# Seven block products instead of eight for half the inner dimension of each MLP's first matrix, in a two-layer decoder trunk

## The chip, the cores and the metric

The kernel runs on one core of a Trainium2 chip. The metric is the device time of one execution in microseconds (us). The engines are TensorE (PE: matmuls; its weight loads are shown apart as PEld), VectorE (DVE), ScalarE (ACT), GpSimd (POOL) and SyncE (SP), whose queue issues most DMAs.

## The reference

Two groups of requests, a prompt of 1024 tokens and 8 x 8 sample tokens, go through two layers with shared weights, in fp32. Layer 0 mixes with gated linear attention (GLA), layer 1 with sliding-window attention; after each mixer comes the MLP that the change touches, then a gated per-layer input embedding (PLE). D_MODEL is 1024, D_FF 4096.

```python
def sq_relu_mlp(hn, w_up, w_down):
    return jnp.square(jax.nn.relu(hn @ w_up)) @ w_down

for i in range(DEPTH):                      # DEPTH = 2
    ...                                     # h = h + mixer(rmsnorm(h, norm_mix[i]))
    h = h + sq_relu_mlp(rmsnorm(h, w['norm_mlp'][i]), w['w_up'][i], w['w_down'][i])
    gate = jax.nn.sigmoid(rmsnorm(h, w['norm_ple'][i]) @ w['w_ple_gate'][i])
    h = h + gate * (p[i] @ w['w_ple'][i])
```

## The kernel before

Both groups are handled together: activations lie transposed, features on the 128 partitions and all T = 1088 tokens along the row. `h` is a list of KT = 8 such tiles, one per 128 features. A row of tokens is cut into the three chunks `CH` of 364, 362 and 362, each of which fits one PSUM buffer. PSUM has three buffers under the tag `mm`, three under `gx` and two under `gs`.

**Precision by three passes.** Every large matmul uses fp32r operands that are split in a high part (a cast on ACT) and a low part (the difference, on DVE). `mm3` (L160 to L165) issues three matmuls, high x high, high x low and low x high. So one 128 x 128 weight block against one chunk is three matmuls, each with its own weight load.

**Weights.** `plan` (L1084) lists all weight tiles in the order of use, each 128 x 512, four 128 x 128 blocks. `wfill` (L115) loads a tile into one of two `raw` buffers, casts it to one of five `hi` buffers (L139) and takes the difference into one of five `lo` buffers (L140). `wnext` (L143) keeps three tiles ahead of the one in use.

**out_proj** (L655) ends the mixer: for each `j` it multiplies, adds the residual to get `h[j]` (L652), adds its square to the norm's sum `acc` (L225, L226), and splits `h[j]` times the gain into a double tile in `hg` (L195 on ACT, L196 on DVE). `norm_end` makes `rb`, the reciprocal norm of each token, through a matmul with ones (L231) and a chain on DVE and ACT (L205 to L210). `rb` is applied after the matmul, so PE can begin the MLP before it is there.

**mlp** (L684) goes over FB = 8 blocks `fb` of the 4096 inner features, FT = 4 tiles of 128 in each. In the up part each `f` is 8 weight blocks x 3 chunks x 3 passes = 72 matmuls; the first `f` of all runs with the weight blocks outermost, so that it asks for the last `hg` late. Each chunk is then evacuated: DVE takes relu times `rb` out of PSUM (L703), ACT squares (L704) and casts (L705), and DVE takes the low part (L706); the result is `u`. In the down part each of eight `j` is 4 blocks x 3 chunks x 3 passes = 36 matmuls, and DVE adds the chunk to `h[j]` (L715). In the last `fb` each `h[j]` is squared, summed and split for the PLE.

**PLE.** A memory pool for its inputs stays open for the whole MLP. At `fb` 2 and 4 `ple_input` (L731) loads one 128 x 1088 tile of `p` each and splits it (L192 on ACT, L193 on DVE). The gate's evacuation (L755) is the first reader of the next `rb`.

**Order.** The program is written as straight code without explicit waits. When it is built, the instructions of each engine are put into one fixed order, by their dependences and by their order in the code, and the waits are added. On the chip each engine then works through its list in that order.

Of the kernel before, what the change touches and what calls it, by code (L numbers as in the profile page):

```python
# [11 lines left out]
F32 = mybir.dt.float32  # L12
F32R = mybir.dt.float32r
U8 = mybir.dt.uint8
AF = mybir.ActivationFunctionType
# [4 lines left out]
P = 128  # L20
# [15 lines left out]
NEG = -1e30  # L36
G_MIX0, G_MLP0, G_PLE0, G_KV, G_MIX1, G_MLP1, G_PLE1, G_FIN = range(8)
WMAX = 544
R = (slice(0, 64), slice(64, 128))


# [5 lines left out]
class Trunk:  # L47
# [67 lines left out]
    def wfill(self, n):  # L115

        while len(self.wtiles) < min(n, len(self.wplan)):
            k, src, width, gains = self.wplan[len(self.wtiles)]
            nc = self.nc
            if src is None:  # L120
                raw = self.rawpair[:, 1, :]
            elif len(src.shape) == 3:
                self.rawpair = self.double("G2", F32)
                self.load(self.rawpair[:, :, :width], src.rearrange("s p w -> p s w"))
                raw = self.rawpair[:, 0, :]
            else:
                raw = self.wp.tile([P, WMAX], F32, tag="raw", name=self.uid("raw"), bufs=2)
                self.load(raw[:, :width], src)
            hi = self.wp.tile([P, WMAX], F32R, tag="hi", name=self.uid("whi"), bufs=5)
            lo = self.wp.tile([P, WMAX], F32R, tag="lo", name=self.uid("wlo"), bufs=5)  # L130
            step = width // len(gains) if gains else width
            for i in range(width // step):
                s = slice(i * step, (i + 1) * step)
                if gains:
                    nc.scalar.activation(hi[:, s], raw[:, s], AF.Copy, scale=gains[i])
                    nc.vector.scalar_tensor_tensor(lo[:, s], raw[:, s], gains[i], hi[:, s].bitcast(F32),
                                                   op0=ALU.mult, op1=ALU.subtract)
                else:
                    nc.scalar.copy(hi[:, s], raw[:, s])  # L139
                    nc.vector.tensor_tensor(lo[:, s], raw[:, s], hi[:, s].bitcast(F32), op=ALU.subtract)  # L140
# [513 lines left out]

    def out_proj(self, key, xs, resid, gain, tags, after=None, begun=0):  # L655
        nc = self.nc
        self.norm_begin()
        self.hg = []
        for j in range(KT):
# [21 lines left out]
        self.norm_end()  # L681


    def mlp(self, layer, gain, utag, tags):  # L684
        nc = self.nc
        xs, rb = self.hg, self.rb
        self.norm_begin()
        self.hg = []
        pt = ("mm", "gx")
        for fb in range(FB):  # L690
            us = []
            if layer == 0:
                self.bias_copies(fb)
            if fb in (2, 4):
                self.ple_input(layer, fb // 2 - 1)
            for f in range(FT):
                ws = self.wtile([("up", layer, fb * FT + f, 0), ("up", layer, fb * FT + f, 1)])
                u = self.double(utag)

                def evac(c0, cn, ps):  # L700
                    s = slice(c0, c0 + cn)
                    t = self.t364()
                    nc.vector.scalar_tensor_tensor(t[:, :cn], ps, 0.0, rb[:, s], op0=ALU.max, op1=ALU.mult)  # L703
                    nc.scalar.activation(t[:, :cn], t[:, :cn], AF.Square)  # L704
                    nc.scalar.copy(u[:, 0, s], t[:, :cn])  # L705
                    nc.vector.tensor_tensor(u[:, 1, s], t[:, :cn], u[:, 0, s].bitcast(F32), op=ALU.subtract)  # L706
                self.gemm(ws, xs, evac, kouter=(fb == 0 and f == 0), tags=pt)
                us.append(u)
# [13 lines left out]
        self.norm_end()  # L722


    def ple_pool(self, layer):
        ctx = ExitStack()
        self.pl = ctx.enter_context(self.tc.tile_pool(name=f"pl{layer}", bufs=1))
        self.p = []
        return ctx
# [354 lines left out]
    def plan(self):  # L1084
# [16 lines left out]
        def rest(layer):  # L1101
# [3 lines left out]
            for j in range(begun, KT):  # L1105
                w.extend(two((f"wo{layer}", j), I[f"w_o{layer}"], j))
            for fb in range(FB):
                for f in range(FT):
                    w.extend(two(("up", layer, fb * FT + f), I["w_up"][layer], fb * FT + f))
# [25 lines left out]
    def run(self):  # L1135
# [7 lines left out]
        def keep(j, h, chunks):  # L1143
# [5 lines left out]
        with self.ple_pool(0):  # L1149
            self.mlp(0, G_PLE0, "G1", ("G2", "G3"))  # L1150
            self.sample_bias()
            self.ple(0, keep)
# [7 lines left out]
        with self.ple_pool(1):  # L1160
            self.mlp(1, G_PLE1, "G2", ("G3", "G1"))
            self.ple(1, scale)


@with_exitstack
# [96 lines left out]
```

## Time and profile before

| | us |
|---|---|
| median of 3 runs | 2738.29 (2736.81 to 2740.18) |
| the profiled execution | 2741.02 |
| its span, first to last instruction | 2738.9 |
| PE busy | 2706.5, 17217 matmuls |
| DVE busy | 1448.5 |
| ACT busy | 1065.8 |
| POOL busy | 128.0 |

The granted TensorE clock is 0.996 of full speed on average. Durations of single instructions can overlap with those of the next on the same engine: the mean durations of a group times its count are then more than its busy time, which counts each moment once. A line of a timeline reads: start, duration, engine, source line, operation, result and operands by name, shape, count, and in brackets the idle time before it and what ended it. A line of a window reads: the stretch, its length, and for each engine its busy time and number of instructions, then the granted clock, the DMA engines' share and GB/s.

### The profile page before, as it was taken

To read this page: it belongs to the slowest core of one execution; us is meant where nothing else is said; L and a number is where in the kernel's file an instruction comes from. 1 tells how busy PE (TensorE), PEld (TensorE's weight loads), DVE (VectorE), ACT (ScalarE), POOL (GpSimd) and SP (SyncE) were. 2 spreads that over 40 slices of the span, in tenths; PEclk is the share of its full clock that TensorE was granted. 3 is DMA by queue.
4 is the path that set the end of the run, shared out by engine and by line. 5 is a ranking of instruction groups with operands and counts; after the bars stand their busy time and mean duration, and the time that the engine had idled before them with its cause. 6 is when DMAs were issued, how large, how long until landed. Compare 5 with 4: busy or idle time off the path is not lost.

```text
span 2738.9 us, 43239 instructions
## 1 busy us (share of the span) xinstructions
PE 2706.5 (99%) x17217; PEld 2639.3 (96%) x17217; DVE 1448.5 (53%) x3481; ACT 1065.8 (39%) x2326; POOL 128.0 (5%) x154
## 2 busy tenths in 40 slices
PE   9999999999999999999999999999999999999997
PEld 8999999999999999999999887899999999999997
DVE  5788786453343343334654677653333333333687
ACT  5565575241122122114434666532221221222465
POOL 0000000001001000010000433200000000000000
PEclk9999999999999999999999999999999999999999
DMA  3121112211111121121122111221111111111152
GB/s 125 40 65 41 57 58 71 90 52 53 53 51 50 45 64 48 49 75 51 56 84 71 41 43 36 70 70 43 47 51 44 46 51 47 43 47 43 36 184 96
DMA packets 92783, 163.34 MB, mean 60 GB/s; under 512 B 11558, under 2 KB 30650, under 8 KB 92549
## 3 DMA queue, kind: packets, MB, share of 16 engines
q1 hardware_dynamic: 89637, 155.20, 18.6%
q10 hardware_dynamic: 1152, 4.46, 0.5%
q8 instruction: 135, 2.21, 0.3%
q0 software_dynamic: 1792, 0.92, 0.2%
q14 instruction: 67, 0.55, 0.1%
HBM read 145.95 MB, written 19.98 MB: 61 GB/s over the span
## 4 chain that ended last, share of the span: by engine, by line
PE 96%; DVE 2%; ACT 1%; issue 0%; DMA 0%; POOL 0%; DVEq 0%; SPq 0%; ACTq 0%; POOLq 0%
PE mm L163 22%; PE mm L164 22%; PE mm L165 22%; PE gx L165 7%; PE gx L164 7%; PE gx L163 7%; PE gx L523 2%; PE gx L1035 1%; PE gx L1021 1%; PE gx L552 1%; PE gx L547 1%; PE gs L1004 1%; PE gs L231 0%; PE gx L554 0%; PE gs L1005 0%
## 5 line engine op out<-in xcount | busy, mean ns | idle before, releaser
L163 PE MATMUL mm<-G,whi 128*128 128x362 f32 (+1 forms) x3416 | 1129.3, 331 | 6.2 <-ACT G L195 6.2
L165 PE MATMUL mm<-G,wlo 128*128 128x362 f32 (+1 forms) x3416 | 1127.7, 330 | 0.1
L164 PE MATMUL mm<-G,whi 128*128 128x362 f32 (+1 forms) x3416 | 1126.3, 330 | 0.0
L163 PEld LDWEIGHTS mm<-G,whi 128*128 128x128 f32 x3416 | 642.9, 188 | 12.7 <-ACT G L195 6.6
L164 PEld LDWEIGHTS mm<-G,whi 128*128 128x128 f32 x3416 | 643.2, 188 | 3.5 <-issue 1.7
L165 PEld LDWEIGHTS mm<-G,wlo 128*128 128x128 f32 x3416 | 642.6, 188 | 3.2 <-issue 1.6
L139 ACT CAST whi<-raw 128x512 fp32r<-128x512 f32 (+1 forms) x368 | 226.4, 619 | 659.1 <-PE mm L164 625.8
L165 PE MATMUL gx<-G,wlo 128*128 128x362 f32 (+1 forms) x1048 | 344.3, 329 | 0.0
L164 PE MATMUL gx<-G,whi 128*128 128x362 f32 (+1 forms) x1048 | 343.8, 328 | 0.0
L163 PE MATMUL gx<-G,whi 128*128 128x362 f32 (+1 forms) x1048 | 343.1, 328 | 0.0
L140 DVE TENSOR_TENSOR wlo<-raw,whi 128x512 fp32r<-128x512 f32 (+1 forms) x368 | 252.0, 690 | 66.1 <-ACT whi L139 65.5
L715 DVE TENSOR_TENSOR H<-H,mm 128x364 f32<-128x364 f32 (+1 forms) x256 | 136.2, 532 | 277.3 <-PE mm L165 276.0
L704 ACT ACTIVATE tmp<-tmp 128x362 f32<-128x362 f32 (+1 forms) x192 | 97.2, 507 | 461.5 <-DVE tmp L703 456.1
L165 PEld LDWEIGHTS gx<-G,wlo 128*128 128x128 f32 x1048 | 198.0, 189 | 0.0
L163 PEld LDWEIGHTS gx<-G,whi 128*128 128x128 f32 x1048 | 197.8, 189 | 0.0
L164 PEld LDWEIGHTS gx<-G,whi 128*128 128x128 f32 x1048 | 197.6, 189 | 0.0
L706 DVE TENSOR_TENSOR G<-tmp,G 128x362 fp32r<-128x362 f32 (+1 forms) x192 | 102.8, 536 | 157.4 <-ACT G L705 157.3
L703 DVE SCALAR_TENSOR_TENSOR tmp<-mm,rb 128x364 f32<-128x364 f32 (+1 forms) x128 | 68.6, 536 | 196.8 <-PE mm L165 196.8
L715 DVE TENSOR_TENSOR H<-H,gx 128x362 f32<-128x362 f32 x128 | 68.0, 531 | 140.9 <-PE gx L165 140.9
L225 ACT ACTIVATE tmp<-H 128x362 f32<-128x362 f32 (+1 forms) x126 | 63.6, 506 | 133.0 <-DVE H L652 74.6
L705 ACT CAST G<-tmp 128x362 fp32r<-128x362 f32 (+1 forms) x192 | 95.0, 496 | 5.8
L226 DVE TENSOR_TENSOR acc<-acc,tmp 128x362 f32<-128x362 f32 (+1 forms) x126 | 67.2, 535 | 36.2 <-ACT tmp L225 35.3
(254 smaller groups left out, 3002.0 us busy)
## 6 DMA issues: line engine op xcount, KB each, us to landing
raw<-in_w_up SPq DMA_DIRECT2D x128, 256.0 KB
raw<-in_w_down SPq DMA_DIRECT2D x128, 256.0 KB
G<-in_w_gate SPq DMA_DIRECT2D x24, 512.0 KB
raw<-in_w_o SPq DMA_DIRECT2D x32, 256.0 KB
raw<-in_w_q SPq DMA_DIRECT2D x24, 256.0 KB
x<-in_xT ACTq DMA_DIRECT2D x8, 544.0 KB
hd<-H SPq DMA_DIRECT2D x8, 544.0 KB
x<-hd SPq DMA_DIRECT2D x8, 544.0 KB
```

The lines of the kernel that those rows point to most:

```text
L139: nc.scalar.copy(hi[:, s], raw[:, s])
L140: nc.vector.tensor_tensor(lo[:, s], raw[:, s], hi[:, s].bitcast(F32), op=ALU.subtract)
L163: mm(out, lhsT=w[0], rhs=x[0], start=first, stop=False)
L164: mm(out, lhsT=w[0], rhs=x[1], start=False, stop=False)
L165: mm(out, lhsT=w[1], rhs=x[0], start=False, stop=last)
L225: nc.scalar.activation(sq[:, :cn], h[:, s], AF.Square)
L226: nc.vector.tensor_tensor(self.acc[:, s], self.acc[:, s], sq[:, :cn], op=ALU.add)
L703: nc.vector.scalar_tensor_tensor(t[:, :cn], ps, 0.0, rb[:, s], op0=ALU.max, op1=ALU.mult)
L704: nc.scalar.activation(t[:, :cn], t[:, :cn], AF.Square)
L705: nc.scalar.copy(u[:, 0, s], t[:, :cn])
L706: nc.vector.tensor_tensor(u[:, 1, s], t[:, :cn], u[:, 0, s].bitcast(F32), op=ALU.subtract)
L715: nc.vector.tensor_tensor(h[:, s], h[:, s], ps, op=ALU.add)
```

## The change

The up matrix of each MLP is no longer done one `f` at a time but in pairs of `f` (`up_pair`). Of the 8 inner blocks `k`, blocks 4 to 7 are multiplied as before. Blocks 0 to 3 go through Strassen's scheme in Winograd's form: the 2 output tiles, the 2 halves of the inner blocks (0, 1 and 2, 3) and the 2 halves of the tokens (HT = 544) form a 2 x 2 x 2 block product of seven products instead of eight. Each half of the tokens is taken in two chunks of CT = 272, one in an `mm` and one in a `gx` buffer.

- **Sums of activations.** `half_sums(i)` forms, for i = 0 and 1, the four sums of the token halves of `h[i]` and `h[i+2]`, split in high and low part, once per layer during out_proj (after `j` = 4 and 6). Three of the four lie in new memory (`st`), one in the second half of `hg[i]`, which therefore is split only for its first half.
- **Sums of weights.** `up_weights` forms the sums of weight blocks from tiles `a1` and `a2` on DVE, two instructions of 256 columns for each of the two sum tiles. The plan has per pair four loaded tiles as before and six split tiles, one of them half as wide: A1, S2S1, C1, S4S3, A22, C2.
- **Sums of products.** The groups of matmuls of a pair are, in order: A1 (12 matmuls), S2S1 (12), A1 and C1 (36), S2S1 (12), S4S3 (12), S4S3 and C1 (36), A22 and C2 (36), C2 (24). Two products are copied to memory on ACT (`p1`, `p5`), three sums are kept in `x`, `u3` and `p5` by DVE, and each `out` adds one of them to its group before relu.
- **Memory.** The sums of products use the buffer `wide` and that of `acc`, so `norm_begin` moves to the last `fb`. The pool for PLE inputs opens only there, in place of `st`, and both `ple_input` follow one another after the last up pair.

The first `f` no longer has a k-outer order. The diff, cut to its core:

```diff
+HT, CT = T // 2, T // 4
@@ wfill
-            if src is None:
+            if isinstance(gains, str):
+                raw, gains = self.up_weights(gains, src), None
+            elif src is None:
@@
+    def up_weights(self, which, src):
+        nc, st = self.nc, self.st
+        q = 2 * P
+        if which == "A1":
+            raw = self.a1 = st.tile([P, 512], F32, tag="a1", name=self.uid("a1"), bufs=1)
+            self.load(raw, src)
+            return raw
+        if which == "A22":
+            return self.a2[:, q:]
+        a1 = self.a1
+        s = st.tile([P, 512], F32, tag="sum", name=self.uid("sum"), bufs=2)
+        if which == "S2S1":
+            a2 = self.a2 = st.tile([P, 512], F32, tag="a2", name=self.uid("a2"), bufs=1)
+            self.load(a2, src)
+            nc.vector.tensor_tensor(s[:, q:], a2[:, :q], a2[:, q:], op=ALU.add)
+            nc.vector.tensor_tensor(s[:, :q], s[:, q:], a1[:, :q], op=ALU.subtract)
+            self.s2 = s
+        else:
+            nc.vector.tensor_tensor(s[:, q:], a1[:, :q], self.a2[:, :q], op=ALU.subtract)
+            nc.vector.tensor_tensor(s[:, :q], a1[:, q:], self.s2[:, :q], op=ALU.subtract)
+        return s
@@ out_proj
-            self.split(d, h, self.gain(gain, j), CH if j >= 6 else ((0, T),))
+            self.split(d, h, self.gain(gain, j), CH if j >= 6 else ((0, HT if j < 2 else T),))
             self.hg.append(d)
+            if j in (4, 6):
+                self.half_sums(j // 2 - 2, gain)
@@
+    def half_sums(self, i, gain):
+        nc = self.nc
+        h1, h2, g1, g2 = self.h[i], self.h[i + 2], self.gain(gain, i), self.gain(gain, i + 2)
+        tiles = [self.hg[i][:, :, HT:]] + [self.st.tile([P, 2, HT], F32R, name=self.uid("tx")) for _ in range(3)]
+        self.tx.append(tiles)
+        for c in (0, CT):
+            n1, n2 = slice(c, c + CT), slice(HT + c, HT + c + CT)
+
+            def part(which, t):
+                d = tiles[which]
+                nc.scalar.copy(d[:, 0, n1], t)
+                nc.vector.tensor_tensor(d[:, 1, n1], t, d[:, 0, n1].bitcast(F32), op=ALU.subtract)
+            t1, t2, b = (self.t364()[:, :CT] for _ in range(3))
+            nc.scalar.activation(b, h1[:, n1], AF.Copy, scale=g1)
+            nc.vector.scalar_tensor_tensor(t1, h1[:, n2], g1, b, op0=ALU.mult, op1=ALU.subtract)
+            part(0, t1)
...
+    def up_pair(self, layer, f, xs, us):
...
+        def out(i, half, x, pss):
+            u = us[i]
+            for c in range(2):
+                s = slice(half * HT + c * CT, half * HT + (c + 1) * CT)
+                t = self.t364()[:, :CT]
+                nc.vector.tensor_tensor(t, x[c], pss[c], op=ALU.add)
+                nc.vector.scalar_tensor_tensor(t, t, 0.0, rb[:, s], op0=ALU.max, op1=ALU.mult)
+                nc.scalar.activation(t, t, AF.Square)
+                nc.scalar.copy(u[:, 0, s], t)
+                nc.vector.tensor_tensor(u[:, 1, s], t, u[:, 0, s].bitcast(F32), op=ALU.subtract)
...
+        a1, s21 = nxt("A1"), nxt("S2S1")
+        ps = bank()
+        add(ps, take(a1, 0), lambda k: (xs[k], 0), True)
+        copies(p1, ps)
+        ps = bank()
+        add(ps, take(s21, 0), lambda k: (tx[k][1], 0), True)
+        sums(x, p1, ps)
+        ps = bank()
+        add(ps, take(a1, 2), lambda k: (xs[k + 2], 0), True, False)
+        c1 = nxt("C1")
+        add(ps, take(c1, 0, 4), lambda k: (xs[k + 4], 0))
+        out(0, 0, p1, ps)
+        ps = bank()
+        add(ps, take(s21, 2), lambda k: (tx[k][0], 0), True)
+        copies(p5, ps)
+        s43 = nxt("S4S3")
+        ps = bank()
+        add(ps, take(s43, 2), lambda k: (tx[k][2], 0), True)
+        sums(u3, x, ps)
+        sums(x, x, p5)
+        sums(p5, p5, u3)
+        ps = bank()
+        add(ps, take(s43, 0), lambda k: (xs[k + 2], HT), True, False)
+        add(ps, take(c1, 0, 4), lambda k: (xs[k + 4], HT))
+        out(0, 1, x, ps)
+        ps = bank()
+        add(ps, take(nxt("A22"), 0), lambda k: (tx[k][3], 0), True, False)
+        c2 = nxt("C2")
+        add(ps, take(c2, 0, 4), lambda k: (xs[k + 4], 0))
+        out(1, 0, u3, ps)
+        ps = bank()
+        add(ps, take(c2, 0, 4), lambda k: (xs[k + 4], HT), True)
+        out(1, 1, p5, ps)
@@ mlp
-        self.norm_begin()
         self.hg = []
+        self.pq = self.wide("pq")
+        self.xz = self.rs.tile([P, TP], F32, tag="acc", name=self.uid("xz"), bufs=1)
...
-            if fb in (2, 4):
-                self.ple_input(layer, fb // 2 - 1)
-            for f in range(FT):
...
+            for f in range(0, FT, 2):
+                us += [self.double(utag) for _ in range(2)]
+                self.up_pair(layer, fb * FT + f, xs, us[f:])
+            if fb == FB - 1:
+                self.norm_begin()
+                self.stx.close()
+                self.ple_open(layer)
```

Left out of the diff are the rest of `half_sums` (three more sums of the same kind), helpers inside `up_pair`, the new lines of `plan`, and `ple_open`, which opens the pool and calls `ple_input` twice.

More of the change, by code (lines that the diff above doesn't have):

```diff
@@ new lines, in up_pair, with bank, take, add @@
+    def up_pair(self, layer, f, xs, us):
+        nc, rb = self.nc, self.rb
+        tx = self.tx
+        def bank():
+            return [self.ps(tag)[:, :CT] for tag in ("mm", "gx")]
+        def take(key, i, count=2):
+            hi, lo = key
+            return [(hi[:, k * P:(k + 1) * P], lo[:, k * P:(k + 1) * P]) for k in range(i, i + count)]
+        def add(pss, ws, x, first=False, stop=True):
+            for c, ps in enumerate(pss):
+                for k, w in enumerate(ws):
+                    d, off = x(k)
+                    off += c * CT
+                    self.mm3(ps, w, (d[:, 0, off:off + CT], d[:, 1, off:off + CT]), first and k == 0,
+                             stop and k == len(ws) - 1)
+        nxt = lambda which: self.wnext(("up", layer, f, which))
+        two = lambda t, i: [t[:, (2 * i + c) * CT:(2 * i + c + 1) * CT] for c in range(2)]
+        p1, p5, x, u3 = two(self.pq, 0), two(self.pq, 1), two(self.xz, 0), two(self.xz, 1)
+        def out(i, half, x, pss):
[8 more added lines that the diff above has]
+                nc.vector.tensor_tensor(u[:, 1, s], t, u[:, 0, s].bitcast(F32), op=ALU.subtract)
+        def copies(t, pss):
+            for c in range(2):
+                nc.scalar.copy(t[c], pss[c])
+        def sums(t, x, pss):
+            for c in range(2):
+                nc.vector.tensor_tensor(t[c], x[c], pss[c], op=ALU.add)
+        a1, s21 = nxt("A1"), nxt("S2S1")
[31 more added lines that the diff above has]
+        out(1, 1, p5, ps)
```

54 lines of the change are left out of this document (30 added, 24 removed).

## The prediction

> **What bounds the kernel now.** I read the page first: its busy times, and its chain of work that ended last.
>
> ```profile
> span 2738.9 us, 43239 instructions
> ...
> PE 2706.5 (99%) x17217; PEld 2639.3 (96%) x17217; DVE 1448.5 (53%) x3481; ACT 1065.8 (39%) x2326; POOL 128.0 (5%) x154
> ...
> PE 96%; DVE 2%; ACT 1%; issue 0%; DMA 0%; POOL 0%; DVEq 0%; SPq 0%; ACTq 0%; POOLq 0%
> ...
> L163 PE MATMUL mm<-G,whi 128*128 128x362 f32 (+1 forms) x3416 | 1129.3, 331 | 6.2 <-ACT G L195 6.2
> ```
>
> 96% of the chain is TensorE (PE), and most of that is the three matmul lines of `mm3`. The MLP is where the change lies, so next come windows over it and over stages that resemble what it will become.
>
> ```profile
> core 0: us, PE busy (x) PEld busy (x) DVE busy (x) ACT busy (x) POOL busy (x), PEclk, DMA share, GB/s
> 942.56:990.40 47.84, 47.84 (x291) 47.84 (x290) 19.18 (x33) 16.86 (x32) 0.00 (x0) 1.00 0.15 45
> 990.40:1038.20 47.80, 47.80 (x289) 47.80 (x289) 17.78 (x32) 5.35 (x9) 6.84 (x12) 1.00 0.21 55
> 65.00:440.00 375.00, 372.53 (x2739) 350.61 (x2738) 301.02 (x1099) 232.68 (x602) 2.84 (x5) 1.00 0.17 54
> 514.00:554.00 40.00, 40.00 (x242) 40.00 (x242) 14.70 (x26) 8.80 (x16) 0.00 (x0) 1.00 0.31 99
> 1278.00:1326.00 48.00, 48.00 (x289) 47.77 (x288) 37.80 (x65) 26.42 (x45) 0.00 (x0) 1.00 0.19 50
> 1719.35:1722.77 3.42, 3.42 (x24) 2.21 (x23) 1.58 (x7) 1.65 (x5) 0.98 (x1) 0.50 0.00 0
> ```
>
> The rows are: an up stage (four `f` of one `fb`), a down stage, the GLA layer, out_proj before the MLP, the last down stage, and a moment of attention. In the MLP PE never pauses, and VectorE (DVE) is busy 19.18 of 47.84 us, 40%. So time falls only if PE does less, and only until DVE or ScalarE (ACT) sets the pace instead.
>
> **The matmuls.** Per pair of `f` the old code issues 2x8x3x3 = 144 matmuls of 362.67 columns on average, 52,224 columns. The new one issues, for its eight groups, 12, 12, 36, 12, 12, 36, 36 and 24 matmuls of 272 columns: 180 matmuls, 48,960 columns, one sixteenth fewer. Whether a matmul is paid by its columns or by the piece decides the gain. 272-column matmuls of the same type stand in the trace: the V projection of head 0 (L389). For the old width I take the evacuations of the first `f` of `fb` 1 and 7.
>
> ```profile
> 37.18 0.29 PE L163 MATMUL mm<-whi,G 128*128 128x272 f32 x1
> ...
> 61.13 0.29 PE L163 MATMUL mm<-whi,G 128*64 128x272 f32 x1
> ```
>
> ```profile
> 659.73 0.54 DVE L703 SCALAR_TENSOR_TENSOR tmp<-mm,rb 128x364 f32<-128x364 f32 x1 [3.44 <-PE mm L165]
> ...
> 1233.77 0.54 DVE L703 SCALAR_TENSOR_TENSOR tmp<-mm,rb 128x364 f32<-128x364 f32 x1 [3.47 <-PE mm L165]
> ```
>
> Between the first two rows lie 8 blocks of 8x3 matmuls: 23.95 us / 192 = 124.7 ns each. Between the second two lie six `fb` of 576 matmuls: 574.04 / 3456 = 166.1 ns. Per column that is 0.4586 and 0.4580 ns: no price per piece is seen. Over two layers of 16 pairs, 4608 x 166.1 = 765.4 us becomes 5760 x 124.7 = 718.5 us: **46.9 us less**. Two neighbouring matmuls of the old width can stand up to 166.7 ns apart, which would make it 50; that is the bound below.
>
> The Trainium skill (TensorE: Matmul & The Clock Gate, "Wait — 56ns, not 53.3ns?") speaks against shorter matmuls: it gives each one columns / 2.4 plus about 2.5 ns. By that the gain would be, as an estimate, 4608 x 153.6 - 5760 x 115.8 = 41 us. The trace, with 0.458 ns per column at both widths, does not agree.
>
> **DVE and ACT per pair.** Prices of single instructions:
>
> ```profile
> L140 DVE TENSOR_TENSOR wlo<-raw,whi 128x512 fp32r<-128x512 f32 x364 | 249.2, 690 | 66.1 <-ACT whi L139 65.5
> ...
> L521 DVE TENSOR_TENSOR E<-E,G 128x128 f32<-128x128 f32 x224 | 50.2, 288 | 8.3 <-ACT E L492 8.3
> L226 DVE TENSOR_TENSOR acc<-acc,tmp 128x362 f32<-128x362 f32 x84 | 44.9, 535 | 24.5 <-ACT tmp L225 23.6
> ...
> L196 DVE SCALAR_TENSOR_TENSOR G<-H,gains,G 128x1088 fp32r<-128x1088 f32 x31 | 42.7, 1382 | 6.5 <-ACT G L195 6.3
> ...
> L196 DVE SCALAR_TENSOR_TENSOR G<-H,gains,G 128x362 fp32r<-128x362 f32 x18 | 10.2, 592 | 1.2 <-ACT G L195 1.2
> ```
>
> ```profile
> L139 ACT CAST whi<-raw 128x512 fp32r<-128x512 f32 x364 | 223.9, 619 | 658.6 <-PE mm L164 625.8 <-DMA raw<-in_w_up 27.4 <-DMA raw<-in_w_q 1.8
> L704 ACT ACTIVATE tmp<-tmp 128x362 f32<-128x362 f32 x128 | 64.7, 507 | 193.1 <-DVE tmp L703 187.7
> L705 ACT CAST G<-tmp 128x362 fp32r<-128x362 f32 x128 | 63.2, 495 | 3.8
> ...
> L1037 ACT COPY H<-gx 128x256 f32<-128x256 f32 x32 | 11.8, 369 | 19.4 <-PE gx L1035 19.0
> ```
>
> On DVE 362 to 512 columns cost 155 ns more, 1.03 ns a column, so 272 cost 442 ns and 256 cost 425. On ACT the step is 0.83 ns: the square 433, the cast 421, the copy out of PSUM 382 ns. DVE per pair: 8 chunks of `out` with three instructions and 8 of `sums` are 32 x 442 = 14.1 us; weights are five low parts of 512 (3.45) and five instructions of 256 (2.1). That is 19.7 us beside 180 x 124.7 ns = 22.4 us of PE: **88%**, from 40%. ACT: 1.5 of copies, 6.8 of `out`, 3.5 of weights: 11.9 us, 53%.
>
> DVE's durations overlap when its work is ready, as this stretch of its timeline shows.
>
> ```profile
> 560.00 0.53 DVE L652 TENSOR_TENSOR H<-mm,x 128x362 f32<-128x362 f32 x1
> 560.44 0.53 DVE L226 TENSOR_TENSOR acc<-acc,tmp 128x362 f32<-128x362 f32 x1
> 560.88 0.59 DVE L196 SCALAR_TENSOR_TENSOR G<-H,gains,G 128x364 fp32r<-128x364 f32 x1
> ...
> 561.84 1.09 DVE L196 SCALAR_TENSOR_TENSOR G<-H,gains,G 128x362 fp32r<-128x362 f32 x2
> ...
> 569.58 0.54 DVE L210 SCALAR_TENSOR_TENSOR rb<-tmp,rb 128x362 f32<-128x362 f32 x1
> ```
>
> Starts are 0.44 us apart at 362 columns, so 0.35 at 272, 0.33 at 256, 0.595 at 512: packed, a pair takes DVE 32 x 0.35 + 3.0 + 1.65 = 15.8 us, 70% of PE's time. The nearest stage is the GLA layer above, with DVE at 301 of 375 us (80%) and PE at 372.5. I therefore cost DVE in steady state at nothing, as long as it need not sit idle inside its own chains. Each group takes one `mm` and one `gx` buffer of three, so a group waits for the first reader of the third before it. The closest are group 6 behind 3 and the next pair's 3 behind 8: 3.0 us for two adds of 0.44. Entering the down stage, the last chunk needs 0.44 + 0.44 + 0.43 + 0.42 + 0.44 = 2.2 us, and 27 matmuls (4.5 us) come before the last `u` is read.
>
> What must not happen is that DVE waits for ACT's square and cast in each chunk with work behind it. These rows show such a wait, and what the order does when chunks come together:
>
> ```profile
> 571.03 0.54 DVE L703 SCALAR_TENSOR_TENSOR tmp<-mm,rb 128x364 f32<-128x364 f32 x1 [0.92 <-PE mm L165]
> 571.53 0.54 DVE L703 SCALAR_TENSOR_TENSOR tmp<-gx,rb 128x362 f32<-128x362 f32 x1
> 572.03 0.54 DVE L703 SCALAR_TENSOR_TENSOR tmp<-mm,rb 128x362 f32<-128x362 f32 x1
> 572.67 0.54 DVE L706 TENSOR_TENSOR G<-tmp,G 128x364 fp32r<-128x364 f32 x1
> ```
>
> ```profile
> 755.42 0.54 DVE L703 SCALAR_TENSOR_TENSOR tmp<-mm,rb 128x364 f32<-128x364 f32 x1 [3.47 <-PE mm L165]
> 757.06 0.54 DVE L706 TENSOR_TENSOR G<-tmp,G 128x364 fp32r<-128x364 f32 x1 [1.10 <-ACT G L705]
> ```
>
> As written, each chunk's L706 stands before the next chunk's L703. At 571 three L703 run first: the order was laid out by readiness, not as written. The idle 1.10 us at 757 has nothing ready behind it.
>
> **The edges of the MLP.** `half_sums` runs twice per layer, each with 16 DVE instructions (eight with a gain at 592 - 90 x 1.088 = 494 ns, eight at 442: 7.5 us) and 12 on ACT (5 us); the two halved splits give back 1.2. Its inputs are `h[0..3]`, early, and its cover is out_proj, where DVE is busy 14.7 of 40 us. If it slipped into the end instead, it would push back the split of `hg[7]`, done at 562.9 above. The new order reads that half about 5 us after PE begins the MLP near 558.6, at 563.5; the margin is under 1 us, where the old k-outer order asked for it last. The norm's `rb` (570.1) no longer holds PSUM, since the new add comes before it. I take 2 us per layer for this edge, from 0 to 7.5.
>
> `ple_input` moves from `fb` 2 and 4 to the end of the ups, into the DVE-heavy last down stage (37.8 of 48 us busy). Per layer it issues two loads, two casts and two subtracts:
>
> ```profile
> L192 ACT CAST p<-praw x4: 1101/1104/1107, 764.9 to 2197.2; 128x1088 fp32r<-128x1088 f32 x4
> L193 DVE TENSOR_TENSOR p<-praw,p x4: 1291/1292/1294, 766.0 to 2198.4; 128x1088 fp32r<-128x1088 f32 x4
> ```
>
> ```profile
> 1332.80 0.54 DVE L210 SCALAR_TENSOR_TENSOR rb<-tmp,rb 128x362 f32<-128x362 f32 x1
> ...
> 1338.38 0.54 DVE L755 TENSOR_TENSOR tmp<-mm,rb 128x364 f32<-128x364 f32 x1 [3.83 <-PE mm L165]
> ```
>
> 2.6 us of DVE fits in the 10 left there; were it late, the gap of 5 us between `rb` and its first reader takes it in layer 0. In layer 1 up to 2.6 us could show. On SyncE's queue the first load waits for `tx` to be freed, the second for the split of the first, and the last down weights queue behind both; three to four of those weights (6 us of PE each) are loaded by then. Nothing is taken for it.
>
> **Sum.** The profiled execution took 2741.0 us (span 2738.9); 2741.0 - 46.9 + 4 = 2698.1. The median of the runs is 2.7 lower: **2695**.
>
> **Rivals.**
> *DVE runs its chains as written* (slower). Each chunk of `out` then occupies DVE for 0.44 + 0.44 + 0.95 idle + 0.44 = 2.3 us; 8 of them, 3.5 of sums and 5.55 of weights are 27.5 us against 22.4. DVE lags 10.2 us per `fb`; the down stage absorbs its 4.5. 16 x 5.7 = 91 us: 2786. It decides once the lag passes 4.5 us per `fb`. The 1.10 us speaks for it, the rows at 571 and the GLA layer against. 0.10. A partial form, a third to two thirds of that loss, gives 2725 to 2756: 0.12.
>
> *Late `half_sums`*: 7.5 us at each of two edges instead of 2 gives 2706, and with the tail's 2.6 some 2709. For it speaks its place behind `j` 4 and 6; against, early inputs and an idle DVE. 0.13.
>
> *The clock.* Only in attention does PE stop often, for up to 1.2 us, and there lies the half-clock window at 1719.35.
>
> ```profile
> PE gx L1021 <- DVE S L986: 2.9, 3, 1.2
> ```
>
> 3.42 us at half speed lose 1.7. Once in every pair that is 55 us: 2750. The Trainium skill (the same page, "A second HAM failure mode: psum-queue depth-cycling") describes this mechanism for groups that cycle through PSUM with short pauses. It needs pauses that the MLP's rows do not have: 0.03.
>
> **How the numbers follow.** The forecast holds 0.62, with its own range 2687 to 2704 (the gain from 50 down, edges 0 to 10). A measurement of this kernel can tell about 0.2%, 5.5 us, from no change. Faster by more: 0.62 + 0.13 + 0.05 of the partial form = 0.80; within: 0.04; slower: 0.16. The range from 2686 reaches through the late sums and the lower partial form to 2735, which leaves out 0.2.
>
> **What would show it.** Right: PE's pitch in an up stage near 124.7 ns, `fb` near 92.7 us (was 95.7), DVE at 70 to 88% there, and PE without waits on DVE. Wrong: idle on PE ahead of the first matmul of a group, released by an add of `out` or a `sums`; PE waiting for `u` at the start of down; DVE idle near 0.95 us before each last subtract with an add ready; a pitch above 128 ns, which alone would take a third of the gain; or a granted clock under 0.98 in the MLP.

## The result and the profile after

| | before | after |
|---|---|---|
| median of 4 runs, us | 2739.15 (2736.81 to 2740.18) | 2709.99 (2708.20 to 2712.72) |
| ratio, 95% interval | | 0.9896 (0.9884 to 0.9908) |
| profiled execution, us | 2741.02 | 2710.06 |
| PE matmuls | 17217 | 18369 |

The kernel is 1.0% faster: 29 us, of 43 forecast. The page of the changed kernel shows the span, then the busy time of each engine, then its chain of work that ended last, by engine.

```profile
span 2708.3 us, 46678 instructions
...
PE 2665.8 (98%) x18369; PEld 2595.9 (96%) x18369; DVE 1735.6 (64%) x4377; ACT 1162.2 (43%) x2694; POOL 127.5 (5%) x154
...
PE 94%; DVE 3%; ACT 2%; issue 0%; DMA 0%; POOL 0%; DVEq 0%; SPq 0%; ACTq 0%; POOLq 0%
```

There are 1152 matmuls more, and PE is busy 40.7 us less: that much of the forecast was there. But PE's share of the span fell from 99% to 98%: its busy time fell 40.7 us and the span only 30.6, so about 10 us of new idle time appeared. Windows over an up stage and the down stage after it, in layer 0 and then in layer 1, say where.

```profile
655.07:702.01 46.94, 45.68 (x361) 45.25 (x361) 32.18 (x77) 20.41 (x49) 0.00 (x0) 1.00 0.17 51
702.01:749.87 47.86, 47.86 (x290) 47.86 (x289) 20.28 (x39) 6.21 (x12) 0.00 (x0) 1.00 0.16 47
1917.41:1962.55 45.14, 45.14 (x361) 45.14 (x361) 32.65 (x77) 20.87 (x49) 0.00 (x0) 1.00 0.19 54
1962.55:2010.41 47.86, 47.86 (x290) 47.86 (x289) 20.29 (x39) 6.22 (x12) 0.00 (x0) 1.00 0.13 39
```

Before, an up stage took 47.84 us in either layer. Layer 1 does it in 45.14, with PE busy throughout; layer 0, with the same matmuls, needs 46.94, and PE is idle in it. The down stages are as they were. So the two layers, alike in arithmetic, got different gains. PE's waits name the difference (the wait, its total, how often, the longest):

```profile
PE mm L189 <- ACT whi L142: 9.5, 8, 1.3
PE mm L189 <- ACT G L221: 6.2, 2, 5.1
PE gs L257 <- DVE acc L252: 3.7, 3, 2.6
```

The first row is new: eight waits for a weight's cast (the high part `whi`), one for each `fb` of layer 0 and none in layer 1. The other two lie elsewhere. Here is ACT's timeline around one of the eight, then PE's, then the same cast on ACT in layer 1.

```profile
669.75 0.43 ACT L772 ACTIVATE tmp<-tmp 128x272 f32<-128x272 f32 x1 [4.74 <-DVE tmp L771]
670.21 0.42 ACT L773 CAST G<-tmp 128x272 fp32r<-128x272 f32 x1
671.49 0.43 ACT L772 ACTIVATE tmp<-tmp 128x272 f32<-128x272 f32 x1 [0.86 <-DVE tmp L771]
671.95 0.42 ACT L773 CAST G<-tmp 128x272 fp32r<-128x272 f32 x1
672.28 0.61 ACT L142 CAST whi<-raw 128x512 fp32r<-128x512 f32 x1
672.80 0.62 ACT L142 CAST whi<-a 128x512 fp32r<-128x512 f32 x1
```

```profile
672.94 0.40 PE L189 MATMUL mm<-G,whi 128*128 128x272 f32 x1 [1.18 <-ACT whi L142]
```

```profile
1921.98 0.62 ACT L142 CAST whi<-raw 128x512 fp32r<-128x512 f32 x1 [2.48 <-DVE sum L165]
```

The cast is that of `C2`, read by the last two groups of the first pair. In layer 1 it comes 4.6 us after the up stage began; in layer 0 17.2 us after it, just as PE needs it. The row at 672.28 has no bracket: ACT was not waiting for the data. The cast stood behind the squares and casts of two outputs (L772, L773), and those waited for DVE; 4.74 us of idle time lie ahead of the first. It is a place in a queue, not a late operand. SyncE's queue shows what layer 0 has and layer 1 has not: a piece of the bias table copy (`ed`) between the loads of `C1` and `C2`, which are the two rows of `raw` here, of the next `fb`.

```profile
716.82 0.33 SPq L78 DMA_DIRECT2D raw<-in_w_up  x1
717.19 0.58 SPq L78 DMA_DIRECT2D ed<-ed  x1
721.38 0.33 SPq L78 DMA_DIRECT2D raw<-in_w_up  x1
```

From the first `ones` matmul of an MLP's norm to that of the next norm, layer 0 went from 767.23 to 760.81 us, layer 1 from 767.40 to 746.04. The missing 15 us are 8 x 1.80 = 14.4 of up stages in layer 0, and little else. The eight waits are 9.5 us of that; the rest lies right behind each of them, where PE also waits for the low part of the same tile and the next matmuls start further apart.

### The profile page after: what moved, and what is told of

Read it like the earlier page. It is cut to its first block, busy times and chain, and to the rows that moved or that the text cites. A ratio compares the mean times of both kernels' runs of the same rounds, so it can differ in the third digit from the quotient of the medians.

```text
span 2708.3 us, 46678 instructions
## 1 busy us (share of the span) xinstructions
PE 2665.8 (98%) x18369; PEld 2595.9 (96%) x18369; DVE 1735.6 (64%) x4377; ACT 1162.2 (43%) x2694; POOL 127.5 (5%) x154
## 3 DMA queue, kind: packets, MB, share of 16 engines
q10 hardware_dynamic: 1152, 4.46, 0.5%
## 4 chain that ended last, share of the span: by engine, by line
PE 94%; DVE 3%; ACT 2%; issue 0%; DMA 0%; POOL 0%; DVEq 0%; SPq 0%; ACTq 0%; POOLq 0%
PE mm L191 20%; PE mm L189 20%; PE mm L190 20%; PE gx L191 8%; PE gx L190 8%; PE gx L189 8%; PE gx L549 2%; PE gx L1162 1%; PE gx L1148 1%; PE gx L578 1%; PE gx L573 1%; PE gs L1131 1%; PE gx L580 0%; PE gs L257 0%; PE gs L1132 0%
## 5 line engine op out<-in xcount | busy, mean ns | idle before, releaser
L189 PE MATMUL mm<-G,whi 128*128 128x362 f32 (+2 forms) x3160 | 1014.2, 322 | 15.7 <-ACT whi L142 9.5
L191 PE MATMUL mm<-G,wlo 128*128 128x362 f32 (+2 forms) x3160 | 1012.6, 320 | 0.8
L190 PE MATMUL mm<-G,whi 128*128 128x362 f32 (+2 forms) x3160 | 1010.8, 320 | 0.0
L189 PEld LDWEIGHTS mm<-G,whi 128*128 128x128 f32 x3160 | 594.8, 188 | 23.6 <-ACT whi L142 11.8
L190 PEld LDWEIGHTS mm<-G,whi 128*128 128x128 f32 x3160 | 594.9, 188 | 3.5 <-issue 1.7
L191 PE MATMUL gx<-G,wlo 128*128 128x272 f32 (+2 forms) x1304 | 397.5, 305 | 0.0
L190 PE MATMUL gx<-G,whi 128*128 128x272 f32 (+2 forms) x1304 | 397.4, 305 | 0.0
L189 PE MATMUL gx<-G,whi 128*128 128x272 f32 (+2 forms) x1304 | 397.1, 305 | 0.0
L190 PEld LDWEIGHTS gx<-G,whi 128*128 128x128 f32 x1304 | 246.1, 189 | 0.1
L189 PEld LDWEIGHTS gx<-G,whi 128*128 128x128 f32 x1304 | 245.9, 189 | 0.1
L772 ACT ACTIVATE tmp<-tmp 128x272 f32<-128x272 f32 x256 | 109.5, 432 | 270.5 <-DVE tmp L771 269.1
L774 DVE TENSOR_TENSOR G<-tmp,G 128x272 fp32r<-128x272 f32 x256 | 111.5, 439 | 59.5 <-ACT G L773 58.7
L771 DVE SCALAR_TENSOR_TENSOR tmp<-tmp,rb 128x272 f32<-128x272 f32 x256 | 110.9, 437 | 3.7
L773 ACT CAST G<-tmp 128x272 fp32r<-128x272 f32 x256 | 106.2, 419 | 5.2
```

What stands on the lines that cost most here:

```text
L189: mm(out, lhsT=w[0], rhs=x[0], start=first, stop=False)
L190: mm(out, lhsT=w[0], rhs=x[1], start=False, stop=False)
L191: mm(out, lhsT=w[1], rhs=x[0], start=False, stop=last)
L771: nc.vector.scalar_tensor_tensor(t, t, 0.0, rb[:, s], op0=ALU.max, op1=ALU.mult)
L772: nc.scalar.activation(t, t, AF.Square)
L773: nc.scalar.copy(u[:, 0, s], t)
```

## The experiments

The theory to be tested: layer 0 loses 1.8 us per `fb` because of the copy between the loads; the rest of the change works as in layer 1. Rivals: something else of layer 0 (its buffers, its inputs); and, for the size of the steady gain, DVE as the hidden bound.

**Copies behind the ups.** In `mlp`, the copies follow both pairs.

```
-            if layer == 0:
-                self.bias_copies(fb)
             for f in range(0, FT, 2):
...
+            if layer == 0:
+                self.bias_copies(fb)
```

> The eight table copies of layer 0 (ed, 384 KB each) are issued after the two up pairs of their fb, not before them. Theory (the fixed order): with a copy ahead of the load of C2 on SyncE's queue, the order of ACT puts the cast of C2 and of the four tiles after it some 12.6 us later than in layer 1, and PE waits for it, though the data is there; the copy itself costs nothing. Then the up stage of layer 0 falls from 46.94 to the 45.15 us of layer 1, the cast of C2 stands about 5 us after the start of each fb, PE's waits for the cast (9.5 us in the profile) go, and the time falls by 8 x 1.8 = 14 us to 2696. Rival (layer 0 differs in its buffers, u in G1 and inputs in G2 and G3): no change, 2710.

Measured: 2716.56 us (2716.32 to 2716.88), ratio 0.9914 (0.9899 to 0.9930). The ups of layer 0 fell to 45.15 us, as the theory had it, but the whole got slower than the changed kernel. Windows over a down stage and an up stage of layer 0, PE's waits, and one wait on PE's timeline:

```profile
605.92:654.89 48.97, 48.08 (x290) 47.77 (x289) 20.80 (x40) 6.70 (x13) 0.00 (x0) 1.00 0.13 44
654.89:700.04 45.15, 45.15 (x363) 45.15 (x362) 32.11 (x76) 20.46 (x48) 0.00 (x0) 1.00 0.18 56
```

```profile
PE mm L189 <- ACT whi L142: 10.0, 1, 10.0
PE mm L191 <- DVE wlo L143: 6.3, 7, 0.9
```

```profile
625.24 0.43 PE L191 MATMUL mm<-G,wlo 128*128 128x364 f32 x1 [0.89 <-DVE wlo L143]
```

The loss moved with the copies, to the weights behind them. Each down stage now waits once for a low part on DVE: two casts of down weights ran on ACT at 608.09, their low parts on DVE only at 624.50, in front of the matmul that needed them. In the last `fb`, where the two cache copies (`kcs`, `vcs`) stand there too, PE waits once for a cast, 10.0 us. ACT's rows put that cast behind the split of the second tile of `p`, which waits for its load:

```profile
1291.43 1.10 ACT L218 CAST p<-praw 128x1088 fp32r<-128x1088 f32 x1 [5.06 <-DMA praw<-in_pT]
1292.43 1.13 ACT L142 CAST whi<-raw 128x512 fp32r<-128x512 f32 x2
```

That load was issued only at 1288 us, when the first tile of `p` had been split, and the last down weights stand behind it on SyncE's queue. The first split ran on ACT at 1285.29 us without waiting for data; in the changed kernel it ran at 1268.26. So this, too, is a changed place in ACT's order. The copy's place decides which data come late; the number that was expected assumed that behind the ups nothing was close, and that was wrong.

**Copies in both layers.** Layer 1 gets copies of its own, of the same shape at the same place, into a scratch table that nothing reads.

```
-            if layer == 0:
-                self.bias_copies(fb)
+            self.bias_copies(fb, layer)
```

> The changed kernel, with copies of the same size and place in layer 1 too, to a scratch table that nothing reads. Theory (the fixed order): the up stages of layer 1 go from 45.15 to about 46.9 us, with the same wait of PE for a cast of C2 once per fb, 8 x 1.8 = 14 us more: 2724. Rival (the buffers of layer 0): no change, 2710, since layer 1 keeps its buffers.

Measured: 2724.27 us (2723.41 to 2726.18), ratio 0.9943 (0.9930 to 0.9957), 14.3 over the changed kernel. An up stage of layer 0, one of layer 1, and PE's longest wait:

```profile
654.49:701.41 46.92, 45.66 (x361) 45.22 (x361) 32.19 (x77) 20.38 (x49) 0.00 (x0) 1.00 0.17 51
1920.47:1967.42 46.95, 45.68 (x361) 45.24 (x361) 32.21 (x77) 20.39 (x49) 0.00 (x0) 1.00 0.17 51
```

```profile
PE mm L189 <- ACT whi L142: 18.8, 16, 1.2
```

Eight waits became sixteen, 9.5 us became 18.8, and layer 1 is now as slow as layer 0. It is the copy, not the layer.

**Only the cast's place.** The copies stay where they are in SyncE's queue; on ACT, the squares of the first two outputs (four chunks) of each `fb` in layer 0 are ordered behind the cast of `C2`.

```
         c1 = nxt("C1")
+        cast = self.cast
...
-                nc.scalar.activation(t, t, AF.Square)
+                r = nc.scalar.activation(t, t, AF.Square)
+                if layer == 0 and f % FT == 0 and i == 0:
+                    self.order(r.ins, cast.ins)
```

`self.cast` is the last weight cast issued, which at that place is the one of `C2`.

> The changed kernel with its copies left between the loads; only ScalarE's order is changed: the squares of the first two output chunks pairs of each block in layer 0 are ordered behind the cast of C2, so the cast stands ahead of them as it does in layer 1. If the late place in the fixed order alone makes the wait (C2's data are there long before): up stages of layer 0 fall to 45.1 to 45.3 us, the time to 2696 (2694 to 2700). If C2's data really land late behind the copy: the cast waits for its load, the squares wait behind it, and the stages take 46.9 us or more, the time 2710 or more.

Measured: 2695.94 us (2694.29 to 2699.17), ratio 0.9842 (0.9827 to 0.9856): 14.05 us faster than the changed kernel, and the best of all versions. A window over an up stage of layer 0, and the cast on ACT's timeline:

```profile
653.08:698.21 45.13, 45.13 (x361) 45.13 (x361) 32.13 (x77) 20.23 (x49) 0.00 (x0) 1.00 0.17 53
```

```profile
662.59 0.62 ACT L142 CAST whi<-raw 128x512 fp32r<-128x512 f32 x1
663.11 0.75 ACT L772 ACTIVATE tmp<-tmp 128x272 f32<-128x272 f32 x2
```

The cast runs 9.5 us after the stage began, ahead of the squares, and waits for no data. The copies move the same bytes on the same queue, and now they cost nothing: it was never the transfer. The two MLPs take 745.85 and 746.06 us, alike.

**Copies by GpSimd.** The same goal by the other way: all copies are issued by GpSimd's queue at their old place in the program.

```
-        self.load(self.ed[s], ...)
+        self.nc.gpsimd.dma_start(self.ed[s], ...)
...
-                self.load(self.O[out][:, 0:120, :], ...)
+                self.nc.gpsimd.dma_start(self.O[out][:, 0:120, :], ...)
```

> The changed kernel with the eight pieces of the table copy (and the two cache copies) issued by GpSimd's queue at the same place in the program, so that they no longer stand between two weight loads of layer 0. Theory (a copy between the loads makes ScalarE's fixed order take the cast of C2 late): all sixteen up stages take 45.1 to 45.2 us, the 1.18 us waits of TensorE for that cast are gone, the down stages stay at 47.85, the time is 2710 - 8 x 1.8 = 2696 (2694 to 2700). Rival (the copies cost by what they move, whoever issues them): layer 0 stays at 46.9 us an up stage, the time at 2710.

Measured: 2701.27 us (2700.35 to 2701.36), ratio 0.9859 (0.9842 to 0.9875), 5 us over what was expected. The ups of layer 0 are right:

```profile
658.53:703.67 45.14, 45.14 (x361) 45.14 (x361) 32.71 (x77) 20.87 (x49) 0.00 (x0) 1.00 0.18 53
```

The rest is at the start of the program, far from the MLP. PE's timeline there, of this kernel and then of the changed one:

```profile
11.55 0.67 PE L189 MATMUL mm<-G,whi 128*128 128x362 f32 x1 [5.78 <-ACT G L221]
```

```profile
6.85 0.67 PE L189 MATMUL mm<-G,whi 128*128 128x362 f32 x1 [1.11 <-ACT G L221]
```

A wait of 1.11 us became 5.78, 4.7 of the 5 us. ACT's row for the split that PE waits for, and a transfer of this kernel (KB, and us from issue to landing), say more:

```profile
10.90 1.08 ACT L221 ACTIVATE G<-H,gains 128x362 fp32r<-128x362 f32 x2 [5.86 <-DMA H<-in_xT]
out_kcs<-in_kpast POOLq DMA_DIRECT2D x1, 960.0 KB, 8.4
```

The split waited for its piece of the input. Beside that load ran the cache copy of `kcs`, 960 KB, which the changed kernel issues on SyncE's queue at 1191 us: on GpSimd's queue it was issued at 2.55 us. So the edit changed the time of this copy with its queue. That the copy held up the input is read off this trace and was not tested by itself.

**The rival, forced.** Every add of `out` and every `sums` is ordered on DVE behind the last subtract of the chunk before it, as the program is written.

```
-                nc.vector.tensor_tensor(t, x[c], pss[c], op=ALU.add)
+                r = nc.vector.tensor_tensor(t, x[c], pss[c], op=ALU.add)
+                if self.lastsub is not None:
+                    self.order(r.ins, self.lastsub)
...
-                nc.vector.tensor_tensor(u[:, 1, s], t, u[:, 0, s].bitcast(F32), op=ALU.subtract)
+                r = nc.vector.tensor_tensor(u[:, 1, s], t, u[:, 0, s].bitcast(F32), op=ALU.subtract)
+                self.lastsub = r.ins
...
```

> The changed kernel, with the first DVE instruction of each chunk of out, and of each sums, ordered behind the last subtract of the chunk before it, as the code is written. The prediction's rival prices this at 5.7 us per fb, 91 us in all, at most: 2710 + 91 = 2801, with DVE idle about 0.95 us before each last subtract. If the fixed order's freedom is not what hides these idle times, because chunks come far enough apart anyhow, it is under 2720.

Measured: 2729.12 us (2725.95 to 2729.46), ratio 0.9957 (0.9944 to 0.9971): 19 us over the changed kernel, not 91, and between the two times that were expected. An up stage of layer 0, one of layer 1, and the down stage behind that:

```profile
659.96:707.35 47.39, 45.66 (x361) 45.22 (x361) 30.28 (x72) 19.75 (x46) 0.00 (x0) 1.00 0.18 51
1934.10:1979.24 45.14, 45.14 (x361) 45.14 (x361) 31.42 (x74) 20.39 (x47) 0.00 (x0) 1.00 0.19 54
1979.24:2027.43 48.19, 48.15 (x290) 47.84 (x289) 21.23 (x42) 7.00 (x14) 0.00 (x0) 1.00 0.11 39
```

In layer 1 the up stage does not move, and the down behind it grows by 0.33 us; that whole MLP takes 749.04 us from norm to norm, 3.0 more than in the changed kernel. Layer 0 loses 14.2 us. PE's waits for the cast of `C2` grew there from 9.5 to 15.3 us, and the granted clock, 1.00 in both MLPs of the changed kernel, fell to 0.50 twice, for 6.83 and 3.41 us; this is the first time:

```profile
579.43:586.26 6.83, 5.63 (x24) 5.63 (x25) 5.76 (x12) 3.29 (x7) 0.00 (x0) 0.50 0.20 47
```

So the price of the chains as written, without a copy between the loads, is the 3.0 us of layer 1. While a chunk of `out` waits for ACT, DVE does low parts and weight sums: they run in the idle time that the rival had counted beside them. The 2.3 us a chunk times 8 are 18.4 us; with eight `sums` at 0.35 that is 21.2 of the 22.6 us that a pair has.

**How much room DVE has.** To the version with the copies on GpSimd's queue, first one and then two products of 128x272 per output chunk were added on DVE, into a scratch tile that nothing reads.

```
+                nc.vector.tensor_tensor(self.scr, rb[:, s], rb[:, s], op=ALU.mult)
                 nc.vector.tensor_tensor(t, x[c], pss[c], op=ALU.add)
```

> The version with the copies on GpSimd's queue, plus one more VectorE product of 128x272 per output chunk, 8 in a pair, into a scratch tile that nothing reads. By the measured busy time (16.3 us a pair) and some 0.36 us from start to start of an instruction: 16.3 + 2.9 = 19.2 us of 22.57, 85%, so no loss: 2696 (within 3). By summed durations (19.7 + 8 x 0.44 = 23.2): 0.6 us a pair over, 32 pairs, about 2716.

> The same with two such products per output chunk, 16 in a pair. By packed time 16.3 + 5.8 = 22.1 us of 22.57, 98%: VectorE is at the edge, any unevenness shows, 2700 to 2730 with up stages of 45.3 to 46.2 us. By summed durations 19.7 + 7.0 = 26.7 us, 4.1 us a pair over: about 2828, up stages of 53 us.

Measured: 2704.49 us (2704.10 to 2707.24) and 2704.34 (2702.58 to 2705.80), 3 us over the version without them, however many there were. (The 2696 that was expected of one product took the version without at 2696; it is at 2701.) The products depend on no chunk, so they did not stay where they were written: they ran ahead, 41 in an early up stage and none in the later ones. Windows over an early down stage and two up stages of the version with two:

```profile
705.63:753.49 47.86, 47.86 (x290) 47.86 (x289) 45.09 (x106) 6.47 (x12) 0.00 (x0) 1.00 0.14 39
753.49:798.73 45.24, 45.24 (x361) 45.24 (x361) 44.46 (x118) 20.60 (x48) 0.00 (x0) 1.00 0.18 54
1912.04:1957.29 45.25, 45.25 (x362) 45.25 (x362) 44.90 (x118) 19.96 (x48) 0.00 (x0) 1.00 0.19 53
```

The test is not the one that was meant, yet it says something stronger: with DVE busy 99% of an up stage, PE does not wait. And durations do not add up: the mean durations of the 118 instructions in the first of these up stages, times their counts, are 53.7 us, in 45.24 us. Of the 3 us, the MLPs have 1.0 (for two products, 746.38 and 746.59 us from norm to norm against 745.88 and 746.07). The rest goes with the clock. Leaving out the end of the program, the profiled executions had a granted clock of 0.50 for 13.7 us with products and 6.8 us without; the difference, at half speed, is up to 3.4 us of lost time by estimate. Half of it is this stretch early in the program, where the version without products has 1.00:

```profile
39.37:42.79 3.42, 3.42 (x13) 3.42 (x12) 3.31 (x9) 2.08 (x6) 1.27 (x2) 0.50 0.70 259
```

Why the clock fell there is not shown. Work that fits anywhere, however, says nothing of work in a chunk's own chain.

**In the chain.** So the products were tied to it, on the version with the cast early: two, then three products that read the chunk right after its add.

```
                 nc.vector.tensor_tensor(t, x[c], pss[c], op=ALU.add)
+                nc.vector.tensor_tensor(self.scr, t, rb[:, s], op=ALU.mult)
+                nc.vector.tensor_tensor(self.scr, t, rb[:, s], op=ALU.mult)
```

> The version with the cast early, plus two VectorE products of 128x272 in each output chunk's own chain (they read the chunk right after its add, so they cannot run ahead of it as the free ones did), 32 in an up stage, into a scratch tile that nothing reads. If instructions overlap as the busy time says (own work 32.7 us of a 45.15 us stage, 0.30 to 0.36 us for each extra one): 42.3 to 44.2 us, 94 to 98%, so up stages of 45.2 to 46 us and 2696 to 2710. If durations add up (39.4 + 32 x 0.437 = 53.4 us): 8.2 us a stage over, 16 stages, about 2828.

> The same with three such products in each chunk's chain, 48 in an up stage. By overlapped time 32.7 + 48 x (0.30 to 0.36) = 47.1 to 50.0 us, 2 to 5 us over what the matmuls take: VectorE is now the bound, TensorE waits for PSUM buffers, up stages of 47 to 50 us, 2726 to 2773. By durations 60.4 us a stage, about 2940. If even this leaves 45.2 us, VectorE's real need is smaller than its busy time says.

Measured: 2711.87 us (2710.58 to 2713.31) and 2723.49 (2721.41 to 2726.80), 16 and 28 us over the version without them. In both, most of it is in layer 0: its MLP takes 14.3 and 23.5 us more than with the cast early, that of layer 1 only 1.3 and 3.3. An up stage of layer 0 with two, then, with three, an up stage of layer 1, the down behind it, an up stage of layer 0, and PE's longest wait:

```profile
655.45:701.91 46.46, 45.51 (x362) 45.29 (x362) 39.88 (x101) 18.99 (x46) 0.00 (x0) 1.00 0.17 52
...
1927.05:1972.30 45.25, 45.25 (x361) 45.25 (x361) 42.40 (x110) 19.28 (x44) 0.00 (x0) 1.00 0.15 48
1972.30:2020.34 48.04, 48.04 (x290) 47.63 (x289) 25.82 (x55) 8.37 (x16) 0.00 (x0) 1.00 0.15 45
657.89:705.06 47.17, 45.51 (x362) 45.29 (x362) 41.14 (x107) 17.62 (x43) 0.00 (x0) 1.00 0.15 46
```

```profile
PE mm L191 <- DVE wlo L143: 14.9, 9, 3.1
```

With two, the ups of layer 1 stayed at 45.24 us, as expected; those of layer 0, behind its first, took 46.4 to 46.5, above what was expected, and the time came out 2 us above its range. With three, DVE was expected to become the bound, at 47 to 50 us a stage; in layer 1 an up stage still takes 45.25. Of its 48 products, 39 ran in it, with DVE 94% busy, and what is left over runs in the down stage, 25.82 us against 20.3: the expectation had weighed the up stage alone. The time came out 2.5 us below its range, and most of the loss has another reason. In layer 0 the stage grew by 2.0 us, and once more PE waits there for a weight: the low part of `C2` on DVE. The edit had brought forward its cast on ACT, not its low part on DVE, and with fuller chains that one came late.

**The price of a piece.** The kernel before, with its up gemm in four chunks of 272 instead of 364, 362 and 362.

```
-                self.gemm(ws, xs, evac, kouter=(fb == 0 and f == 0), tags=pt)
+                self.gemm(ws, xs, evac, kouter=(fb == 0 and f == 0), tags=pt,
+                          chunks=tuple((272 * c, 272) for c in range(4)))
```

> The kernel before, with the up part in four chunks of 272 tokens instead of three of 364, 362 and 362: the same columns in 6144 matmuls instead of 4608, and 8 evacuations per pair instead of 6. By columns alone: no change, 2739, and 124.7 ns a matmul. With 2.5 ns for each matmul: 1536 x 2.5 = 3.8 us more, 2743. DVE stays far below PE, at about 45%, so it should not show.

Measured: 2747.46 us (2745.49 to 2748.83), ratio 1.0025 (1.0016 to 1.0034): 7.6 us slower than before, twice what the higher of the two expectations had. An up stage of layer 0 and one of layer 1:

```profile
655.94:704.21 48.27, 48.27 (x385) 48.27 (x385) 19.31 (x40) 17.59 (x39) 0.00 (x0) 1.00 0.15 45
1934.33:1982.59 48.26, 48.26 (x385) 48.26 (x385) 19.31 (x39) 17.68 (x38) 0.00 (x0) 1.00 0.14 39
```

The same columns in 384 matmuls instead of 288 take some 48.25 us instead of 47.84, with PE never idle: 125.6 ns for each. Sixteen stages are 6.6 of the 7.6 us. A piece does have a price in this stage.

## Why the prediction was right, and where its sizes were off

The forecast was faster, 2695 in a range from 2686 to 2735; the kernel is faster, at 2710. It came out at the forecast's own number only with the cast early (2695.94). That agreement is partly luck: two of its terms were off by some 4 us each, and they cancel.

**The matmuls: right in kind, 3.8 us too large.** An up stage of layer 1 gives 45.14 / 360 = 125.4 ns a matmul where the prediction took 124.7, from the V projection. So 765.4 - 5760 x 0.1254 = 43.1 us were to be had, not 46.9. The mistaken reading was "no price per piece is seen": 124.7 came from another stage with other operands, and 0.7 ns in 5760 matmuls is 4 us. The four-chunk experiment shows the price with only the chunks changed: a straight line through 166.1 ns at 362.67 columns and 125.6 at 272 leaves 0.447 ns a column and about 4 ns for each matmul. (It has two evacuations more in a pair, for which PE does not wait.) The rule that the prediction set aside (the Trainium skill, TensorE: Matmul & The Clock Gate, "Wait — 56ns, not 53.3ns?": columns / 2.4 plus about 2.5 ns) was the better guide to the difference: the estimate by it was 41 us, and 43.1 were measured; the times that it gives, 115.8 ns at 272 columns, are under the 125.4 measured here.

**DVE at nothing: right.** PE has no wait on DVE in the up stages of layer 1. DVE is busy 32.65 of 45.14 us there, 72%, near the packed estimate (70%) and not the sum of durations (88%). The close agreement is partly luck: seven of the 84 instructions that both counted ran in the down stage (39 there, 32 before), and the 77 that stayed took 0.42 us of busy time each, where the packed estimate had 0.38. DVE reached 0.38 only when it was full, with two free products: 118 instructions in 44.46 us. The experiments show the room directly: with 39 more instructions in the chains, an up stage of layer 1 grew by 0.11 us.

**The edges: 2 us a layer expected, close to nothing found.** With the cast early the MLPs went from 767.23 and 767.40 us to 745.85 and 746.06, by 21.4 and 21.3 us; eight up stages at 47.84 - 45.15 = 2.69 are 21.5. The prediction expected `half_sums` early in out_proj's idle time. DVE's timeline of the changed kernel, with the first and the last row of the second of them in layer 0, then the split of `hg[7]` and the last `rb`:

```profile
548.93 0.50 DVE L730 SCALAR_TENSOR_TENSOR tmp<-H,gains,tmp 128x272 f32<-128x272 f32 x1
...
560.50 0.43 DVE L727 TENSOR_TENSOR tx<-tmp,tx 128x272 fp32r<-128x272 f32 x1
...
562.69 1.09 DVE L222 SCALAR_TENSOR_TENSOR G<-H,gains,G 128x362 fp32r<-128x362 f32 x2
...
571.14 0.53 DVE L236 SCALAR_TENSOR_TENSOR rb<-tmp,rb 128x362 f32<-128x362 f32 x1
```

It ran into the very end of out_proj, the case that a rival had at 7.5 us an edge. The split came 0.85 us later than before, `rb` 1.56 later; PE waited 0.25 us, before a `ones` matmul. So the event of that rival came true and its price did not: a delay of DVE's work is not a delay of PE's. `ple_input` in the last down stage, forecast at nothing, showed no wait of PE either; that this hangs on the order, too, is seen in the version with the copies behind the ups, where it led to the wait of 10.0 us.

**SyncE's queue at nothing: this is the term that was mis-sized.** The prediction wrote of `ple_input`'s loads and found nothing to charge; of the copies in `bias_copies`, which stand among the new up loads in layer 0 alone, it said nothing. That is the 14.4 us, and its mechanism was on no list: not a late transfer, nor a late DVE, but a changed place of one cast in ACT's fixed order. Nothing in the trace of before shows such a wait in the MLP; that the order is laid out by readiness was read off the rows at 571, and it was applied to DVE only, where it helped.

**The rivals.** DVE's chains as written, priced at 91 us, cost 19 when forced, 3.0 of them in layer 1, whose up stage stayed as it was. The clock stayed: 1.00 in both MLPs, 0.997 over the span. As a danger it was real: in the MLPs of versions with longer waits it fell to 0.50 for 3.4 to 10.2 us. One slip in the forecast's own range changes nothing: 2741.0 - 50 - 2.7 is 2688, not 2687.

**The signs.** The pitch was under 128 ns, DVE between 70 and 88%, and no wait on DVE appeared. An `fb` of 92.7 us was expected; layer 1 has 45.14 + 47.86 = 93.0, layer 0 94.8. That last number, read by layer, is the sign that found the fault.

**What stays open.** That the copy moves the cast in ACT's order, and that the place in the order makes the wait, is shown from both sides. By which estimate the order is laid out was only seen, not traced. That the early copy of `kcs` put 4.7 us at the start of the program, and why the granted clock fell in the versions with free products, was not tested.

## What to carry to other kernels

When a change gains in one layer and less in its twin, compare the twins by stage before anything else: the difference here was one 0.6 us cast, and its cure (an order for that one instruction) was worth half of what the whole rewrite had brought. A wait whose releaser did not itself wait for data is a question of order on that engine: look at what stands ahead of it, and at what changed on the queue that feeds it. Take the price of an instruction from the same stage if 0.5% of it matters, and where there is none, measure the old work in the new size.

## What the runs showed of the hardware

- Matmuls back to back took 166.1 ns at 362.67 columns on average and 125.4 to 125.6 at 272 in the same stage, PE never idle: 0.447 ns a column and about 4 ns for each, by a line through the two.
- DVE instructions of 272 columns last 0.44 us each, yet 118 instructions with 53.7 us of durations ran in 45.24 us: on that engine the busy time, not the sum of durations, says what room is left.
- Eight table copies of 384 KB between weight loads on one queue cost nothing by themselves (45.13 us an up stage with the cast early, 45.14 without any copy), while their place moved 14 us.
- The granted clock was 1.00 in both MLPs of the changed kernel, where PE's waits in the up stages were 1.3 us at most. It fell to 0.50 in layer 0's MLP, for 3.4 us where the longest wait was 3.1 (three products), and for 10.2 us where it was 3.7 (chains as written) and 10.0 (copies late).
